# Third slots for attention scores and transposed probabilities, six temporaries, and a 1 KB transfer scratch in a five-layer transformer kernel

## The chip, the cores and the metric

One core of a Trainium2 chip runs the whole program. The metric is the device time of one execution, in microseconds; the number to compare is the median of three runs of each kernel.

## What is computed

The input is one sequence of 512 tokens with 1024 channels in float32. Four layers with post-normalisation run first: latent attention (MLA), sliding-window attention (SWA), attention with forget gates (FOX) and MLA again. A fifth, larger block follows: a short convolution, a pooling mixer, two kinds of attention with relative bias (one with a top-k choice of keys), a gated feed-forward part and a gated projection at the end.

```python
for i in range(4):                       # MLA, SWA, FOX, MLA
    y = branch[i % 3](x)                 # (softmax(q k^T) v * silu(gate)) @ w_out
    x = layernorm(ALPHA * x + y)
x = x + rmsnorm(concat(conv, pool, topk_attn, block_attn) @ w_out_2)
x = x + rmsnorm(swiglu(rmsnorm(x)))
x = x + sigmoid(rmsnorm(x) @ w_ple_gate) * (p @ w_ple_proj)
```

Each attention has 16 heads of 64 value channels in the first four layers; MLA and FOX are causal over all 512 keys, SWA sees the block before and its own.

## The kernel before, in words

Every float32 operand of a large matmul is split into a high and a low part (`split`, L183; `w`, L131, for weights), and a product is three matmuls, L157 to L159 (`mm3`). Weights come in pieces of 256 KB by DMA, issued by SyncE; ScalarE makes the high part (L138), GpSimd or VectorE the low part (L139).

A layer of the first four runs over eight pairs of heads (`pairs`, L586). For each pair the projections of the *next* pair are written first (`prep`), then the two heads of this pair, then its gate (L601), then the product of gate and result (`gated`, L465: og times u, a cast L469, a low part L470). After the eight pairs `layer_end` (L304) multiplies by the output weights, normalises and transposes; the output weights borrow free tiles: `f` for the last two pieces of the first half (L263), `qk` and one `pth`/`ptl` for the second half (`pair_units`, L266).

One head is `attend` (L390). TensorE makes the scores in PSUM tiles "s" (L157 to L159 for MLA, L238 and L239 otherwise). VectorE adds the mask or bias and finds the row maximum (L403), which writes the scores into one SBUF tile with tag "p", up to 1280 numbers a partition. ScalarE takes the exponential in place (L419), VectorE the reciprocal (L422) and the normalisation in place (L427). TensorE transposes 128x128 blocks into PSUM tiles "t" (L443), ScalarE casts them into "pth" (L184), VectorE makes "ptl" (L185), and TensorE multiplies both with the values into the PSUM tile "o" (L452). `join` (L458) adds the two halves of "o" into a tile "og" with tag "f" (L462, L463). So "p" is held from the first L403 of a head to its last L443.

Tags stand for a fixed number of slots: a tile waits until one of its tag's slots is free. The first four layers share one pool with the counts of `PH1`; the fifth block has two pools (`PH2`, `PH3`) that lie over the same memory afterwards. PSUM has 3 "acc", 2 "s", 2 "t" and 1 "o". The order of instructions on each engine is not the written order: the framework's planner (`schedule_with_timeline_sim=True`, L1133) arranges it before the run by its own timing model, from the dependences, the written order as priority and the free slots. On the chip each engine then follows that order.

```python
PS_BUFS = dict(acc=3, s=2, t=2, o=1)
sc = s.t("p", [P, sum(w)])               # L396, held to the last transpose
nc.tensor.transpose(ps[:, n:n + P], sc[:, c:c + P], s.ident)   # L443
ph = s.t("pth", [P, S], R)               # L445
```

Of the kernel before, what the change touches and what calls it, by code (L numbers as in the profile page):

```python
# [88 lines left out]
class Kern:  # L89
# [993 lines left out]
    def run(s, x, out, layers=range(4), second=True):  # L1083
        with ExitStack() as ctx:
            s.phase(ctx, PH1)
            xT = s.act(8)
# [15 lines left out]
            s.ple(hT, out)  # L1102


PH1 = dict(cqt=1, f=4, p=2, pth=2, ptl=2, qk=7, qr=1, cq=2, ckv=2, rope=2, kr=1, gq=1)
PH2 = dict(kl=2, f=6, p=2, pth=2, ptl=2, v=3, qk=4, rb=2, cw=6, pad=3, bd=2, iw=1, sel=1, sb=1, m8=3)
PH3 = dict(f=6, p=2, hid=6, hid2=2, sel=1, sb=1)

# [28 lines left out]
```

## Time and profile before

| what | us |
|---|---|
| median of 3 runs (1758.92 to 1761.11) | 1760.01 |
| the profiled execution | 1762.84 |
| its span, first to last instruction | 1761.1 |
| TensorE (PE) busy | 1684.8 |
| VectorE (DVE) busy | 962.0 |
| ScalarE (ACT) busy | 873.8 |
| GpSimd (POOL) busy | 854.4 |
| mean granted clock of TensorE | 0.979 of full |

A row of the profile names an engine, a line of the kernel and the tiles (written <- read). PE are matmuls, PEld weight loads, which run beside them. Busy time of PE is modelled from the size of each matmul, and one matmul overlaps the next, so the distance from start to start is the better measure of pace. "Idle before" is time in which the engine did nothing before an instruction, with what ended it. In the first four layers the stages are: start and latents of MLA 0 to 70 us, its heads 70 to 252, the layer's end and the projections of SWA to 316, its heads to 478, the layer's end and start of FOX to 546, its heads to 777, the same for MLA to 868, its heads to 1043, and the layer's end with the start of the fifth block to 1101.

### The profile page before, as it was taken

The page shows a single profiled execution, that of the slowest core. Times are in us where ns is not written, and L with a number is a line of the kernel's source. Part 1 is how long each engine was busy: PE and PEld are TensorE (multiplying, and loading weights), DVE is VectorE, ACT ScalarE, POOL GpSimd, SP SyncE. Part 2 cuts the span into 40 slices and gives each one's busy share as a digit, 9 for nine tenths or more (in the row PEclk, how much of TensorE's full clock was granted, in tenths as well). Part 3 has the DMA queues.
Part 4 walks back from the last instruction along what each step waited for, and adds up shares of the span by engine and source line. Part 5 has one row for each costly group of instructions (what it writes and reads, how often), then busy time and mean ns, then how long its engine had stood idle before and what let it go on. Part 6 is the DMA issues. An engine that isn't in the chain of part 4 may idle for free.

```text
span 1761.1 us, 25691 instructions
## 1 busy us (share of the span) xinstructions
PE 1684.8 (96%) x8818; PEld 1435.2 (81%) x8818; DVE 962.0 (55%) x2223; ACT 873.8 (50%) x2054; POOL 854.4 (49%) x775
## 2 busy tenths in 40 slices
PE   8999999999999999999999998999999999999999
PEld 7888878887788888778888877877778888888877
DVE  4587654677654665766587665599544222210053
ACT  4576543666445655633576642755544333332351
POOL 1644534444255665616644523745644444443571
PEclk9999999999999999999999998999999999999999
DMA  5434534322032333314444523332332333332332
GB/s 169 132 98 114 165 104 124 99 70 87 26 97 81 101 88 93 116 51 127 120 110 103 176 61 74 91 81 64 114 90 83 98 96 96 96 100 80 105 99 72
DMA packets 190339, 173.91 MB, mean 99 GB/s; under 512 B 14280, under 2 KB 154952, under 8 KB 190208
## 3 DMA queue, kind: packets, MB, share of 16 engines
q1 hardware_dynamic: 190208, 172.27, 33.9%
q8 instruction: 70, 1.15, 0.3%
q14 instruction: 61, 0.50, 0.1%
HBM read 150.94 MB, written 6.87 MB: 90 GB/s over the span
## 4 chain that ended last, share of the span: by engine, by line
PE 52%; DVE 9%; ACT 2%; issue 2%; POOL 2%; DMA 1%; SPq 0%; ACTq 0%; POOLq 0%; DVEq 0%
PE ps_acc L157 11%; PE ps_acc L158 11%; PE ps_acc L159 11%; PE ps_s L158 4%; PE ps_s L157 4%; PE ps_s L159 4%; PE ps_o L452 2%; PE ps_t L443 2%; DVE p L427 1%; DVE sel L926 1%; ACT p L419 1%; DVE m L925 1%; DVE p L403 1%; PE ps_s L238 1%; DVE ptl L185 1%
## 5 line engine op out<-in xcount | busy, mean ns | idle before, releaser
L139 POOL TENSOR_TENSOR wl<-wr,wh 128x512 fp32r<-128x512 f32 (+2 forms) x362 | 472.7, 1316 | 421.5 <-ACT wh L138 408.7
L138 ACT CAST wh<-wr 128x512 fp32r<-128x512 f32 (+2 forms) x368 | 223.6, 613 | 364.9 <-PE ps_acc L158 125.1
L157 PE MATMUL ps_acc<-act,wh 128*128 128x512 f32 (+1 forms) x880 | 331.5, 377 | 0.9 <-DVE v L620 0.8
L158 PE MATMUL ps_acc<-act,wh 128*128 128x512 f32 (+1 forms) x880 | 330.2, 375 | 0.3 <-DVE act L185 0.2
L159 PE MATMUL ps_acc<-act,wl 128*128 128x512 f32 (+1 forms) x880 | 330.1, 375 | 0.0
L157 PEld LDWEIGHTS ps_acc<-act,wh 128*128 128x128 f32 x880 | 165.6, 188 | 27.9 <-PE ps_acc L159 1.2
L159 PEld LDWEIGHTS ps_acc<-act,wl 128*128 128x128 f32 x880 | 165.3, 188 | 27.5
L158 PEld LDWEIGHTS ps_acc<-act,wh 128*128 128x128 f32 x880 | 165.4, 188 | 27.0 <-DVE act L185 0.7
L419 ACT ACTIVATE p<-p,st 128x256 f32<-128x256 f32 (+3 forms) x288 | 153.5, 537 | 32.8 <-DVE st L410 17.3
L157 PE MATMUL ps_acc<-wh,act 128*128 128x256 f32 (+3 forms) x384 | 134.5, 350 | 7.7 <-ACT act L469 3.1
L185 DVE TENSOR_TENSOR ptl<-ps_t,pth 128x512 fp32r<-128x512 f32 (+1 forms) x200 | 117.6, 597 | 38.5 <-ACT pth L184 37.7
L184 ACT CAST pth<-ps_t 128x512 fp32r<-128x512 f32 (+1 forms) x200 | 100.3, 516 | 72.5 <-PE ps_t L443 63.0
L443 PE MATMUL ps_t<-c_ident,p 128*128 128x128 f32 x672 | 116.9, 283 | 17.3 <-DVE p L427 12.4
L427 DVE TENSOR_SCALAR p<-p,st 128x256 f32<-128x256 f32 (+3 forms) x264 | 132.1, 559 | 1.8
L159 PE MATMUL ps_acc<-wh,act 128*128 128x256 f32 (+3 forms) x384 | 130.7, 341 | 0.1
L158 PE MATMUL ps_acc<-wl,act 128*128 128x256 f32 (+3 forms) x384 | 130.4, 340 | 0.0
L443 PEld LDWEIGHTS ps_t<-c_ident,p 128*128 128x128 f32 x672 | 82.0, 143 | 33.7 <-DVE p L427 13.2
L452 PE MATMUL ps_o<-pth,v 128*128 128x256 f32 (+3 forms) x288 | 90.1, 318 | 6.3 <-DVE og L463 4.4
L452 PE MATMUL ps_o<-ptl,v 128*128 128x256 f32 (+3 forms) x288 | 88.2, 335 | 4.3 <-DVE ptl L185 4.2
L157 PEld LDWEIGHTS ps_acc<-wh,act 128*128 128x128 f32 x384 | 77.8, 203 | 16.0 <-ACT act L469 3.3
L158 PEld LDWEIGHTS ps_acc<-wl,act 128*128 128x128 f32 x384 | 77.7, 202 | 5.1 <-issue 0.5
L159 PEld LDWEIGHTS ps_acc<-wh,act 128*128 128x128 f32 x384 | 77.1, 201 | 5.5 <-DVE act L185 0.3
(371 smaller groups left out, 3801.3 us busy)
## 6 DMA issues: line engine op xcount, KB each, us to landing
wr<-in_w_gate_up_dram SPq DMA_DIRECT2D x88, 256.0 KB, 2.8
wr<-in_fox_w_in_dram SPq DMA_DIRECT2D x60, 256.0 KB, 3.1
wr<-in_w_in_dram SPq DMA_DIRECT2D x48, 256.0 KB, 2.9
wr<-in_w_down_dram SPq DMA_DIRECT2D x44, 256.0 KB, 2.6
wr<-in_swa_w_in_dram SPq DMA_DIRECT2D x40, 256.0 KB, 2.9
wr<-in_mla_w_in_dram SPq DMA_DIRECT2D x32, 256.0 KB, 3.1
qk<-qk SPq DMA_DIRECT2D x32, 256.0 KB, 3.1
wr<-in_mla_w_out_dram SPq DMA_DIRECT2D x32, 256.0 KB, 3.5
```

Of the source, the lines that this page charges most:

```text
L138: nc.scalar.copy(h, raw)
L139: (nc.vector if dve else nc.gpsimd).tensor_sub(l, raw, h.bitcast(F32))
L157: mm(out, lh, rh, start=first, stop=False)
L158: mm(out, lh, rl, start=False, stop=False)
L159: return mm(out, ll, rh, start=False, stop=last)
L184: s.nc.scalar.copy(hi, src)
L185: s.nc.vector.tensor_sub(lo, src, hi.bitcast(F32))
L238: mm(out, q[:, e, c], kd[:, kk], start=True, stop=False)
L419: nc.scalar.activation(a, a, AF.Exp, bias=st[:, 1, i:i + 1], scale=scale, accum_out=st[:, 2, i:i + 1])
L427: nc.vector.tensor_scalar_mul(a, a, st[:, 3, i:i + 1])
L443: nc.tensor.transpose(ps[:, n:n + P], sc[:, c:c + P], s.ident)
L452: nc.tensor.matmul(o[:, j * P:j * P + m], vj, pp[:, c:c + m], start=first, stop=k == 1 and grp[-1] == max(2, grp[-1]) and j == grp[-1], sk ...
```

## The change

The counts of the first pool grow: `f` from four to six slots, `p`, `pth` and `ptl` from two to three. The room is taken from the reserve that the framework keeps in each SBUF partition for transfers whose addresses are computed on the way: it falls from the framework's default of 16,384 bytes to 1024. The functions of the kernel are unchanged.

```diff
-PH1 = dict(cqt=1, f=4, p=2, pth=2, ptl=2, qk=7, qr=1, cq=2, ckv=2, rope=2, kr=1, gq=1)
+PH1 = dict(cqt=1, f=6, p=3, pth=3, ptl=3, qk=7, qr=1, cq=2, ckv=2, rope=2, kr=1, gq=1)
...
-    nc = bacc.Bacc("TRN2", target_bir_lowering=False, num_devices=1)
+    nc = bacc.Bacc("TRN2", target_bir_lowering=False, num_devices=1, dynamic_dma_scratch_size=1024)
```

A slot of `f`, `pth` and `ptl` is 2 KB a partition, a slot of `p` 5 KB.

## Rows read from the trace of the kernel before

**Rows 1.** The page's part 1: busy time, share of the span and instructions of each engine.

```profile
PE 1684.8 (96%) x8818; PEld 1435.2 (81%) x8818; DVE 962.0 (55%) x2223; ACT 873.8 (50%) x2054; POOL 854.4 (49%) x775
```

**Rows 2.** Busy time by stage of the first 1101 us: stretch (us from the span's start), its length, then busy us and instructions (x) of PE, PEld, DVE, ACT and POOL, the mean granted clock of TensorE, DMA share and GB/s.

```profile
0.00:70.00 70.00, 60.60 (x344) 54.72 (x344) 30.11 (x66) 34.29 (x95) 29.96 (x43) 0.98 0.49 149
70.00:252.00 182.00, 172.93 (x935) 147.18 (x933) 127.94 (x347) 113.85 (x301) 84.94 (x78) 0.98 0.45 124
252.00:316.00 64.00, 63.00 (x371) 54.51 (x372) 29.96 (x56) 24.90 (x45) 28.07 (x21) 0.97 0.42 125
316.00:478.00 162.00, 151.82 (x796) 127.62 (x795) 119.86 (x331) 99.18 (x262) 61.10 (x47) 0.96 0.23 68
478.00:546.00 68.00, 67.12 (x410) 59.62 (x409) 33.89 (x62) 29.69 (x57) 39.29 (x39) 1.00 0.32 91
546.00:777.00 231.00, 223.45 (x1240) 193.18 (x1238) 147.60 (x368) 138.78 (x332) 127.14 (x127) 0.98 0.32 92
777.00:868.00 91.00, 87.72 (x476) 77.19 (x476) 48.15 (x88) 33.99 (x96) 54.19 (x60) 0.98 0.37 107
868.00:1043.00 175.00, 168.71 (x921) 143.54 (x919) 124.31 (x342) 109.37 (x293) 73.45 (x67) 0.99 0.43 120
1043.00:1101.00 58.00, 49.85 (x297) 45.14 (x298) 35.65 (x59) 17.36 (x36) 22.89 (x23) 0.91 0.26 64
```

**Rows 3.** Waits of PE over the whole span: who waited for whom, us in total, times, longest us.

```profile
PE ps_t L443 <- DVE p L427: 12.4, 17, 2.5
PE ps_acc L157 <- ACT act L469: 7.3, 3, 3.1
PE ps_s L238 <- DVE st L403: 5.5, 7, 1.6
PE ps_t L443 <- DVE ptl L185: 4.5, 6, 2.4
PE ps_o L452 <- DVE og L463: 4.4, 10, 0.9
PE ps_o L452 <- DVE ptl L185: 4.2, 4, 2.7
```

**Rows 4.** Timeline of one place in the heads of SWA: start us, us, engine, line, operation, tiles, shape, count, and in brackets the idle time before it with what ended it.

```profile
429.31 3.12 DVE L427 TENSOR_SCALAR p<-p,st 128x128 f32<-128x128 f32 x4
429.46 1.29 POOL L139 TENSOR_TENSOR wl<-wr,wh 128x512 fp32r<-128x512 f32 x1 [1.36 <-ACT wh L138]
...
430.95 0.44 PE L443 MATMUL ps_t<-c_ident,p 128*128 128x128 f32 x2 [0.49 <-DVE p L427]
...
432.23 0.70 PE L443 MATMUL ps_t<-c_ident,p 128*128 128x128 f32 x4 [0.84 <-DVE p L427]
...
434.52 0.33 PE L238 MATMUL ps_s<-qk 128*128 128x128 f32 x1 [1.18 <-DVE st L403]
```

**Rows 5.** The stretch after that place by busy time (columns as in rows 2), and from the timeline two weight matmuls in it and two some 38 us earlier.

```profile
434.80:441.40 6.60, 6.45 (x16) 4.81 (x16) 2.78 (x10) 2.17 (x9) 0.00 (x0) 0.50 0.40 119
...
437.15 0.63 PE L157 MATMUL ps_acc<-wh,act 128*128 128x512 f32 x1
437.58 0.63 PE L158 MATMUL ps_acc<-wl,act 128*128 128x512 f32 x1
...
398.55 0.39 PE L157 MATMUL ps_acc<-act,wh 128*128 128x512 f32 x1
398.78 0.39 PE L158 MATMUL ps_acc<-act,wh 128*128 128x512 f32 x1
```

**Rows 6.** Timeline around the first reduction of a head in the first MLA layer, in FOX and in the second MLA layer.

```profile
90.67 0.38 PE L443 MATMUL ps_t<-c_ident,p 128*128 128x128 f32 x2
91.24 0.68 DVE L403 CUSTOM_DVE_ANT_0 p<-ps_s,c_mask 128x512 f32<-128x512 f32 x1
...
686.08 0.38 PE L443 MATMUL ps_t<-c_ident,p 128*128 128x128 f32 x2
686.86 0.68 DVE L403 CUSTOM_DVE_ANT_0 p<-ps_s,rope 128x512 f32<-128x512 f32 x1
...
980.93 0.33 PE L159 MATMUL ps_s<-qk 96*128 96x384 f32 x1
982.48 0.39 PE L443 MATMUL ps_t<-c_ident,p 128*128 128x128 f32 x2
982.90 0.69 DVE L403 CUSTOM_DVE_ANT_0 p<-ps_s,c_mask 128x512 f32<-128x512 f32 x1 [0.38 <-PE ps_t L443]
```

**Rows 7.** Waits of DVE over the whole span: reductions that waited for transposes.

```profile
DVE p L403 <- PE ps_t L443: 7.2, 8, 1.9
```

**Rows 8.** The page's part 3: the queue that carries the kernel's own transfers, and the two of instructions.

```profile
q1 hardware_dynamic: 190208, 172.27, 33.9%
q8 instruction: 70, 1.15, 0.3%
q14 instruction: 61, 0.50, 0.1%
```

**Rows 9.** Waits of all engines over the whole span: two around borrowed tiles.

```profile
ACT pth L138 <- PE ps_o L452: 14.9, 5, 4.9
POOL f L139 <- DVE og L463: 14.0, 2, 8.5
```

**Rows 10.** Busy time in a stretch of the feed-forward part, columns as in rows 2.

```profile
1364.00:1584.00 220.00, 220.00 (x973) 182.15 (x972) 46.80 (x59) 71.70 (x121) 104.75 (x81) 1.00 0.33 97
```

## The prediction

> **What bounds the kernel now.** I read the page first, then busy time and clock by stage, then TensorE's waits, then single heads in the timeline. On the page TensorE (PE) is busy for 96% of the span and no other engine for over 55% [rows 1]. A gain can therefore only come from what PE loses between its matmuls, and the change can reach PE's losses only in the first four layers, whose pool it enlarges. The table by stage shows where they are [rows 2]. In the four attention stretches PE stands idle for 182 − 172.93 = 9.1 us, 162 − 151.82 = 10.2, 231 − 223.45 = 7.6 and 175 − 168.71 = 6.3: together 33 us. In the same rows the granted clock lies below 1; (1 − clock) times length gives 3.6 + 6.5 + 4.6 + 1.8 = 16.5 us of lost clock. The projections between them lose little: 1.0, 0.9 and 3.3 us.
>
> PE's own list of waits says for what [rows 3]. The longest one is for the transposes of a head's probabilities, which wait for VectorE's normalisation (L427): 12.4 us in 17 waits. The scores (L238) wait 5.5 us for VectorE's reduction (L403) to empty a PSUM bank. Then come waits at which SBUF slots play no part: the output projection waits for the last head's gated product (7.3 us), and heads wait for the PSUM tiles "o" and "t" (4.4 and 4.5 us).
>
> The timeline of one place in the sliding-window layer shows how such a wait goes on [rows 4]. Four normalisations take 3.12 us beside work of GpSimd, PE's transposes wait 0.49 and 0.84 us between them, the next scores wait 1.18 us, and from there to 441.4 the clock granted is 0.50, that is 1.2 GHz: two matmuls of 128x512 start 0.43 us apart, against 0.23 us at 2.4 GHz [rows 5].
>
> What ties two neighbouring heads together is the tag "p". A head keeps its slot from its first reduction to its last transpose, and there are two. In three heads of three layers the pattern is the same [rows 6]: the last transposes of the head before the previous one run at 90.67, 686.08 and 982.48, and the first 512-wide reduction of the new head starts 0.57, 0.78 and 0.42 us later, although in the third case its scores had left PE by 981.3. As a wait that VectorE shows, this is small (7.2 us in 8 waits [rows 7]); the planner, which orders the instructions before the run, has put other work there. It costs through the order: while a head is held back, PE has one chain fewer to turn to when the normalisation of the older one is late.
>
> **The change part by part.** *Scratch.* All of the kernel's own transfers are issued by SyncE and appear on the one queue "hardware_dynamic", with 190,208 packets; the other queues carry instructions only [rows 8]. No transfer that GpSimd would build is in the trace, so the smaller scratch takes nothing away: 0 us. It frees 15 KB a partition, and the new slots need 2 x 2 KB (f), 5 KB (p, 1280 numbers) and 2 x 2 KB (pth, ptl), 13 KB in all. No instruction or transfer is added or removed; what moves is the planned order.
>
> *Third slot of p.* It can act on the waits of L443 for L427 and of L238 for L403: 12.4 + 5.5 = 17.9 us. It shortens no chain; it gives PE another head's scores to run while one waits, and it does so only where slots were the limit, as in the three heads. The long wait chosen above lies beside a busy GpSimd and stays as long as it is, if nothing else is at hand. I take half, 9 us; bounds 0 and 17.9 for a gain, and a loss under the rivals.
>
> *Clock.* The 16.5 us come with such waits, but not only with these: the stretch of rows 5 has three of them ahead of it. I take a third, 5.5 us; bounds 0 and 16.5.
>
> *Third slots of pth and ptl.* The casts into pth (L184) wait for the transposes, which is for data. In the list a slot of pth is waited for only where the output weights borrow it (L138 behind L452, 14.9 us in 5 waits of ScalarE [rows 9]), and at that time PE has the other weights at hand. 0 us, at most the 4.2 us that L452 waits for ptl [rows 3].
>
> *Six f.* At a layer's end the last two weight pieces borrow four f, which is all there are; GpSimd then stands 14.0 us in 2 waits behind the last head's join [rows 9]. PE there waits for the gated product (7.3 us), which is late for its own chain. So 0 us; if more early gate projections were to leave PE without filling at a layer's end, the cost would be seen there.
>
> *What comes back.* Heads that follow closer press on the same one bank of "o" and two of "t", whose waits are 4.4 + 4.5 = 8.9 us now; a quarter more is +2 us (bounds 0 and 8.9).
>
> *Later stages.* The second pool's tiles lie over other tiles of the first; the hand-over, 1043 to 1101, has 8.2 us of PE idle and a clock of 0.91 [rows 2], and its waits are for the normalised rows. 0 us, ±3.
>
> Sum: −9 − 5.5 + 2 = −12.5 us. The profiled execution took 1762.8 us (span 1761.1, 1.7 outside it), 2.8 over the median of the three runs. The saving is taken off the median: 1760.0 − 12.5 = **1747.5 us**.
>
> **Weighed against a page.** In the stretch 1364 to 1584 PE has no wait at all, and its weight loads (PEld) take 182.15 of 220 us, 82.8% [rows 10]; in the attention stretches they take 80.9, 78.8, 83.6 and 82.0% [rows 2]. If that share were the ceiling, the room would be 3.5 + 6.5 + 0 + 1.4 = 11.4 us, idle and clock together, not the 49.6 counted above. The Trainium skill (Perfetto Trace Analysis, Identifying the Most-Contended Engine) holds the busy share of matmuls a poor measure and wants headroom judged by the busy share of weight loads; no row here shows which of the two is right where short transposes are mixed in. With half of 11.4 the sum would be −5.7.
>
> **The rivals.**
> *Slower: the order on VectorE.* VectorE works in the planned order. With a third slot, four reductions of a new head (0.68 us for the first, rows 6) can stand ahead of the normalisation for which PE waits. For: VectorE is at 127.94 of 182 and 119.86 of 162 us in these stretches [rows 2] and each such wait reaches PE; the planner decides by its own durations, and the 3.12 us of rows 4 are not typical. Against: older work should come first where both are ready. It decides from the point where this happens at each of the 17 waits: 17 x 0.68 = 11.6 us, and one more stretch at 1.2 GHz such as that of rows 5 (6.6 us at half, 3.3 lost): +15, **1775 us**.
> *No difference: PSUM.* The tags acc, s, t and o hold 3 + 2 + 2 + 1 tiles. A new head's scores need a free s, its result the only o, and both stay as they are. For: the waits for banks, 5.5 + 4.5 + 4.4 = 14.4 us, are above the 12.4 for the normalisation [rows 3], and VectorE seldom waits for a slot outright [rows 7]. Then the third slots lie unused: **1760 us**. The Trainium skill (Perfetto Trace Analysis, Optimization Strategy) says that bubbles which repeat can mean SBUF or PSUM is short; it does not tell which.
> *Small gain: weight loads.* The ceiling of the part before: 1760.0 − 5.7, **1754 us**.
>
> **How the numbers follow.** Forecast 0.45, weight loads 0.15, PSUM 0.16, order on VectorE 0.24. A measurement of this kernel can tell about 0.2% from no change, 3.5 us. So faster 0.60, same 0.16, slower 0.24. The range begins at all of the 17.9 us and half of the clock with nothing given back, −26: 1734. Above, it takes in PSUM and half of the loss on VectorE, +8: 1768. Left out are the rest of that loss (0.1) and clock gains beyond the half. The likeliest case alone runs from 1734 to 1756.
>
> **What would show it.** Right: in the profile after, L443's waits for L427 at 4 to 8 us, attention stretches shorter by 2 to 5 us each, sliding-window most, clock there 0.97 and up, first reductions that no longer follow the transposes of the head two before, and no change from 1364 on. Wrong: the same PE waits under another name (o, t or s banks), which is PSUM; L443's waits longer, with reductions between L422 and L427, which is VectorE; layer ends longer by what the attention saved, which would mean that filling was only used up earlier.

## The result, and the profile after

The changed kernel takes 1780.97 us (median of 4 runs, 1778.31 to 1781.87) beside 1759.47 for the kernel before: a ratio of 1.0122 [1.0104, 1.0140]. It is 21 us slower, where 12.5 less were forecast. Its profiled execution took 1781.87 us with a span of 1780.1, 19.0 more than the span before.

Page of the kernel after: the span, part 1 and the queue of the kernel's own transfers.

```profile
span 1780.1 us, 25673 instructions
...
PE 1686.4 (95%) x8818; PEld 1437.5 (81%) x8818; DVE 943.7 (53%) x2223; ACT 873.5 (49%) x2054; POOL 851.8 (48%) x775
...
q1 hardware_dynamic: 190208, 172.27, 33.9%
```

Work and transfers are those of before [rows 1, 8]. PE's busy time grew by 1.6 us and its idle time from 1761.1 − 1684.8 = 76.3 to 93.7 us, so idle time is 17.4 of the 19.0.

The kernel after by stage, cut at its own boundaries; columns as in rows 2.

```profile
0.00:74.00 74.00, 62.16 (x353) 55.71 (x353) 31.23 (x69) 34.27 (x95) 33.73 (x47) 1.00 0.51 150
74.00:256.00 182.00, 171.21 (x924) 146.06 (x924) 121.00 (x343) 113.84 (x301) 81.80 (x75) 0.98 0.45 122
256.00:320.00 64.00, 62.62 (x370) 54.70 (x371) 29.84 (x56) 24.77 (x45) 26.20 (x20) 0.97 0.40 119
320.00:486.00 166.00, 153.36 (x801) 129.39 (x799) 118.13 (x331) 99.19 (x263) 62.34 (x48) 0.95 0.23 68
486.00:555.00 69.00, 65.97 (x404) 58.78 (x405) 34.03 (x62) 29.26 (x56) 37.67 (x38) 1.00 0.31 85
555.00:787.00 232.00, 223.74 (x1240) 193.50 (x1238) 142.22 (x368) 139.46 (x333) 129.42 (x128) 0.98 0.34 93
787.00:880.00 93.00, 87.66 (x466) 77.03 (x467) 46.98 (x87) 33.41 (x95) 50.72 (x58) 0.96 0.33 99
880.00:1062.50 182.50, 171.29 (x930) 145.93 (x928) 121.35 (x344) 109.73 (x294) 75.61 (x69) 0.98 0.43 116
1062.50:1120.00 57.50, 48.78 (x302) 44.04 (x303) 35.70 (x59) 17.06 (x36) 22.45 (x22) 0.94 0.25 65
```

What was 1101 us is now 1120, and what follows is 660.1 us in both (1761.1 − 1101 and 1780.1 − 1120): the whole loss lies in the first four layers and the hand-over. Length minus PE's busy time in the four attention stretches was 33.2 us [rows 2] and is 10.8 + 12.6 + 8.3 + 11.2 = 42.9. The rest of the 17.4 lies at the layer ends (0.4, 2.2 and 2.1), the start (2.4) and the hand-over (0.6). The clock is no better: (1 − clock) times length gives 3.6 + 8.3 + 4.6 + 3.7 = 20.2 us in these stretches, after 16.5.

Waits of PE in the kernel after, over the whole span (columns as in rows 3).

```profile
PE ps_s L238 <- DVE st L403: 9.3, 11, 2.7
PE ps_t L443 <- DVE ptl L185: 8.7, 7, 2.5
PE ps_acc L157 <- ACT act L469: 8.1, 4, 2.8
PE ps_t L443 <- DVE p L427: 7.7, 9, 1.9
...
PE ps_o L452 <- DVE og L463: 5.8, 7, 1.2
PE ps_o L452 <- ACT pth L184: 5.5, 5, 2.3
...
PE ps_o L452 <- DVE ptl L185: 4.1, 5, 2.7
...
PE ps_s L157 <- DVE st L403: 1.0, 4, 0.3
```

Set beside rows 3, the wait for the normalisation fell from 12.4 to 7.7 us. The waits for banks of PSUM rose: those for "s" from 5.5 to 9.3 + 1.0, for "t" from 4.5 to 8.7, for "o" from 4.4 to 5.8. The products that wait for the cast L184 went from 1.8 (below the rows shown of before) to 5.5. Together 14.1 us came and 4.7 went. (These waits are of the whole span; the four attention stretches hold most of them.)

The tie that the prediction read from rows 6 is gone for most heads. Counted from the start of a head's first L403 and the end of its last L443, 35 of the 56 heads that have two heads before them in their layer start while both of these are still open; in the kernel before it is none. Timeline of the first MLA layer after: the first reduction of a head here runs 4.8 us ahead of the last transposes of the head two before it.

```profile
87.59 0.69 DVE L403 CUSTOM_DVE_ANT_0 p<-ps_s,c_mask 128x512 f32<-128x512 f32 x1
...
89.67 1.27 DVE L427 TENSOR_SCALAR p<-p,st 128x128 f32<-128x128 f32 x4
...
92.38 0.38 PE L443 MATMUL ps_t<-c_ident,p 128*128 128x128 f32 x2
```

One place in SWA shows what PE waits for instead. Timeline of the kernel after; columns as in rows 4.

```profile
396.17 0.42 DVE L403 CUSTOM_DVE_ANT_0 p<-ps_s,win 128x256 f32<-128x256 f32 x1
...
397.14 0.81 PE L443 MATMUL ps_t<-c_ident,p 128*128 128x128 f32 x6
...
397.72 0.36 PE L238 MATMUL ps_s<-qk 128*128 128x256 f32 x1
...
401.55 0.61 ACT L469 CAST act<-og 128x512 fp32r<-128x512 f32 x1
401.57 4.10 DVE L427 TENSOR_SCALAR p<-p,st 128x128 f32<-128x128 f32 x4
401.72 1.26 POOL L139 TENSOR_TENSOR wl<-wr,wh 128x512 fp32r<-128x512 f32 x1 [2.82 <-ACT wh L138]
402.18 0.97 ACT L184 CAST pth<-ps_t 128x512 fp32r<-128x512 f32 x2
402.82 0.54 PE L452 MATMUL ps_o<-pth,v 128*128 128x256 f32 x1 [2.32 <-ACT pth L184]
402.94 1.31 POOL L470 TENSOR_TENSOR act<-og,act 128x512 fp32r<-128x512 f32 x1
...
404.22 1.30 POOL L139 TENSOR_TENSOR wl<-wr,wh 128x512 fp32r<-128x512 f32 x1
405.60 0.41 DVE L403 CUSTOM_DVE_ANT_0 p<-ps_s,win 128x256 f32<-128x256 f32 x1
...
406.07 0.47 PE L238 MATMUL ps_s<-qk 128*128 128x128 f32 x1 [2.71 <-DVE st L403]
```

And the stretch around it by busy time (columns as in rows 2).

```profile
400.00:407.00 7.00, 1.97 (x8) 1.25 (x6) 5.77 (x12) 4.11 (x12) 3.81 (x3) 0.71 0.17 52
407.00:413.00 6.00, 5.57 (x31) 4.92 (x30) 5.23 (x16) 3.69 (x9) 0.00 (x0) 0.77 0.08 29
```

The transposes end at 397.95, but their casts start at 402.18, behind the exponentials of the next head, a weight cast and the gated product's cast on ScalarE: the first 2.32 us. Then the next head's scores wait 2.71 us for a bank "s", whose reduction stands behind 4.10 us of the older head's normalisation on VectorE. PE works for 1.97 of 7 us, and the clock granted is 0.71 and 0.77 in these two rows. The head whose scores of 397.72 hold that bank was begun at 396.17, while the two heads before it were still open, so it had taken a third slot; that gave PE nothing to do here. The wait is for one bank: the trace shows no access to the other "s" between 396.8 and 406.07, and why the waiting scores were not given that one is open.

### The profile page after: what moved, and what is told of

Its sections match the earlier page's. It is cut to its first block, busy times and chain, and to the rows that moved or that the text cites. A ratio compares the mean times of both kernels' runs of the same rounds, so it can differ in the third digit from the quotient of the medians.

```text
span 1780.1 us, 25673 instructions
## 1 busy us (share of the span) xinstructions
PE 1686.4 (95%) x8818; PEld 1437.5 (81%) x8818; DVE 943.7 (53%) x2223; ACT 873.5 (49%) x2054; POOL 851.8 (48%) x775
## 4 chain that ended last, share of the span: by engine, by line
PE 53%; DVE 8%; issue 3%; POOL 2%; ACT 2%; DMA 1%; SPq 0%; POOLq 0%; DVEq 0%; ACTq 0%
PE ps_acc L157 11%; PE ps_acc L158 11%; PE ps_acc L159 11%; PE ps_s L157 4%; PE ps_s L158 4%; PE ps_s L159 4%; PE ps_o L452 2%; PE ps_t L443 2%; DVE sel L926 1%; DVE p L427 1%; DVE m L925 1%; DVE p L403 1%; ACT p L419 1%; PE ps_s L238 1%; PE ps_s L239 1%
## 5 line engine op out<-in xcount | busy, mean ns | idle before, releaser
L157 PE MATMUL ps_acc<-act,wh 128*128 128x512 f32 (+1 forms) x880 | 332.4, 378 | 1.1 <-DVE f L606 0.9
L157 PEld LDWEIGHTS ps_acc<-act,wh 128*128 128x128 f32 x880 | 166.1, 189 | 28.4 <-DVE f L606 1.1
L185 DVE TENSOR_TENSOR ptl<-ps_t,pth 128x512 fp32r<-128x512 f32 (+1 forms) x200 | 117.1, 597 | 47.2 <-ACT pth L184 46.4
L157 PE MATMUL ps_acc<-wh,act 128*128 128x256 f32 (+3 forms) x384 | 131.0, 341 | 7.2 <-ACT act L469 2.8
L184 ACT CAST pth<-ps_t 128x512 fp32r<-128x512 f32 (+1 forms) x200 | 98.8, 519 | 72.5 <-PE ps_t L443 67.1
L159 PE MATMUL ps_acc<-wh,act 128*128 128x256 f32 (+3 forms) x384 | 128.9, 336 | 0.4 <-DVE act L185 0.4
L443 PE MATMUL ps_t<-c_ident,p 128*128 128x128 f32 x672 | 110.7, 282 | 16.8 <-DVE ptl L185 8.7
L427 DVE TENSOR_SCALAR p<-p,st 128x256 f32<-128x256 f32 (+3 forms) x264 | 123.0, 526 | 1.7
L443 PEld LDWEIGHTS ps_t<-c_ident,p 128*128 128x128 f32 x672 | 81.2, 144 | 29.4 <-issue 12.3
L157 PEld LDWEIGHTS ps_acc<-wh,act 128*128 128x128 f32 x384 | 76.1, 198 | 14.8 <-ACT act L469 3.0
L463 DVE TENSOR_TENSOR og<-ps_o,og 64x512 f32<-64x512 f32 x72 | 49.0, 681 | 59.1 <-ACT og L462 58.2
```

The lines of the kernel that those rows point to most:

```text
L157: mm(out, lh, rh, start=first, stop=False)
L159: return mm(out, ll, rh, start=False, stop=last)
L184: s.nc.scalar.copy(hi, src)
L185: s.nc.vector.tensor_sub(lo, src, hi.bitcast(F32))
L427: nc.vector.tensor_scalar_mul(a, a, st[:, 3, i:i + 1])
L463: nc.vector.tensor_add(og[a], o[:64], og[a])
```

## The experiments

The theories go by numbers in the expectations. T1: the third slot of p opens further heads, and VectorE then stands in the join (VectorE's wait of L463 behind L462 is 12.7 us before the change and 58.2 after). T2: any new order costs, whatever the cause. T3: six f use up filling early. T4: pth and ptl carry the loss. T5: TensorE's order carries it. T6: ScalarE's does. T7: no single engine's does. T8: only slots of the chain of heads (f, p, pth, ptl) cost. T9: the further heads wait for the PSUM tiles s, t and o. T10: the new order is bad whatever the banks.

**Each part alone.** Four kernels, each with the scratch of 1024 bytes:

```diff
-    nc = bacc.Bacc("TRN2", target_bir_lowering=False, num_devices=1)
+    nc = bacc.Bacc("TRN2", target_bir_lowering=False, num_devices=1, dynamic_dma_scratch_size=1024)
# scratch_only: this alone; the others, beside it, in PH1:
# p3_only: p=3      f6_only: f=6      pt3_only: pth=3, ptl=3
```

scratch_only: 

> Only the 1 KB scratch; all slot counts as before. The planned order of every engine is the same as before, only addresses differ. Both theories (T1: the third p slot; T2: any new order costs a few us) expect no change: ratio 0.998 to 1.002. If it is slower by 1%, the memory placement or the scratch is the cause and both fall.

p3_only: 

> 1 KB scratch and p=3; f, pth, ptl as before. T1 (a third scores slot lets the planner open another head ahead, heads get longer from first reduction to join, VectorE stands in the join L463 behind ScalarE's L462, TensorE loses that): nearly the whole loss, +14 to +22 us (1774 to 1782), the wait of L463 for L462 at 40 us or more against 12.7 before. T2 (each new order costs or gains a few us in an unrelated way): anything from -8 to +12 us, and the wait of L463 does not follow the time.

f6_only: 

> 1 KB scratch and f=6; p, pth, ptl as before. T1: 0 to +4 us. T3 (early gate projections use up the filling of TensorE): +8 to +20 us. T2: anything from -8 to +12.

pt3_only: 

> 1 KB scratch and pth=ptl=3; p and f as before. T1: within 4 us of before, L463's wait for L462 stays near 13 us. T4 (a third pth and ptl lets transposes run ahead of the one PSUM tile o, so that joins come later): +8 to +20 us with L463's wait at 30 us or more. T2: anything from -8 to +12.

| kernel | median us | ratio to before (1760.07) |
|---|---|---|
| scratch_only | 1761.37 | 1.0009 [0.9993, 1.0025] |
| p3_only | 1770.57 | 1.0053 [1.0035, 1.0071] |
| f6_only | 1764.05 | 1.0030 [1.0009, 1.0051] |
| pt3_only | 1768.80 | 1.0045 [1.0032, 1.0058] |

The scratch costs nothing that can be measured. Each group of slots costs something of its own, 0.53 + 0.30 + 0.45 = 1.28% against 1.22 for all: no one part carries the loss. T1 wanted 1774 to 1782 from the third p alone and nothing from pth and ptl, and missed both. T3's 8 to 20 us from six f did not come (4.0). T4's forecast for pth and ptl came true (+8.7 us, and VectorE's wait of L463 for L462 at 43.4 us), but p alone costs as much, so T4 falls as the whole cause. T2's wide range holds all three. Waits of PE with the third p alone, then with the third pth and ptl alone:

```profile
PE ps_o L452 <- DVE ptl L185: 7.8, 7, 2.7
PE ps_t L443 <- DVE ptl L185: 7.4, 4, 2.9
PE ps_s L238 <- DVE st L403: 5.9, 7, 2.9
...
PE ps_t L443 <- DVE p L427: 4.5, 7, 1.0
```

```profile
PE ps_o L452 <- DVE ptl L185: 10.4, 13, 2.7
PE ps_t L443 <- DVE ptl L185: 8.6, 6, 2.6
PE ps_t L443 <- DVE p L427: 6.1, 10, 0.9
```

Both cut the wait for the normalisation and lengthen those for the casts' second half (L185) and the bank "t", which L185 empties; rows 3 have 4.2 and 4.5 for these two. With the third p alone the two waits that were to shrink fell from 17.9 to 4.5 + 5.9 = 10.4 us, and the kernel still became slower. With the third pth and ptl alone no head starts on a third slot (0 of 56, after 33 with the third p alone): waits grow there although no more than two heads are open at once.

**The slots with the old order, and one engine held.** The program is planned twice: first with the old slots, to learn each engine's order, then with the new ones, where every instruction of a held engine is chained to the one before it in the old order. The chain is an order of issue without a wait on the chip. In the traces the held orders of TensorE, VectorE and ScalarE are those of before in every place.

```diff
+OLD = dict(PH1, f=4, p=2, pth=2, ptl=2)
+NEW = dict(OLD, f=6, p=3, pth=3, ptl=3)
+PINNED = ('PE', 'DVE', 'Activation', 'Pool', 'SP')      # order_old: all five
...
+            for name in order:
...
+                if e in last:
+                    tc.add_manual_dep(i, last[e], mybir.DependencyInfo(mybir.DependencyClass.NoSync, ...
+                last[e] = name
# pin_pe: ('PE',)   pin_dve: ('DVE',)   pin_dve_act: ('DVE', 'Activation')   pin_act: ('Activation',)
# free_act, free_dve, free_pe: all five but that one
```

order_old: 

> All slots of the changed kernel and the 1 KB scratch, but the instructions of all five engines held in the order that the planner found with the old slot counts. If the loss lies in the new order alone (T1 and T2 alike): 1752 to 1764 us, ratio 0.996 to 1.002; the reductions can no longer wait for a slot of p (7.2 us in 8 waits before), so at best a few us are gained. If the slots themselves cost (placement in memory, later stages laid over other tiles): 1770 or more.

pin_pe: 

> Changed slots; only TensorE's order held as before, the other four engines are ordered anew. T1 (the loss comes from the order of VectorE and ScalarE, with joins standing early in their queues): 1770 to 1780, L463's wait for L462 at 35 us or more. T5 (the loss comes from TensorE's order: further heads are begun and the filling is spent early): 1755 to 1765, whatever L463 waits.

pin_dve: 

> Changed slots; only VectorE's order held as before. T1: 1756 to 1765 and L463's wait for L462 back under 20 us. T5: 1770 or more, since TensorE's order differs in thousands of rows.

pin_dve_act: 

> Changed slots; VectorE's and ScalarE's order held as before, TensorE free (its order then differs in far fewer rows). T1: 1756 to 1764. T5: 1762 to 1772, between before and changed.

free_act: 

> Changed slots; TensorE, VectorE, GpSimd and SyncE hold the order of before, only ScalarE is ordered anew. T6 (ScalarE's order carries the loss: with a third pth the casts of transposes and the copies of the join stand ahead of work that is ready, and ScalarE waits at the head of its queue): 1768 to 1780. T7 (no single engine carries it, each engine's new order costs some): 1762 to 1768. If ScalarE is innocent: 1756 to 1762.

pin_act: 

> Changed slots; only ScalarE's order held as before, the other four ordered anew. T6: 1757 to 1766, against 1781 to 1784 with only TensorE or only VectorE held. T7: 1768 to 1782.

free_dve: 

> Changed slots; TensorE, ScalarE, GpSimd and SyncE hold the order of before, only VectorE is ordered anew. If VectorE's order alone carries the loss (reductions of further heads ahead of other work): 1770 to 1782. If it takes the new orders of several engines together: 1757 to 1765, as with only ScalarE anew (1760.8).

free_pe: 

> Changed slots; only TensorE is ordered anew, within what the held orders of the other four allow (its order then differs in some 790 rows). If TensorE's order carries the loss by itself: 1766 to 1776. If it takes several engines together: 1757 to 1764.

(The kernel before had medians of 1761.61, 1760.95 and 1760.65 beside them.)

| kernel | held in the old order | median us | ratio to before |
|---|---|---|---|
| order_old | all five | 1757.99 | 0.9981 [0.9969, 0.9993] |
| free_act | all but ScalarE | 1760.80 | 1.0005 [0.9989, 1.0021] |
| free_dve | all but VectorE | 1762.25 | 1.0016 [1.0002, 1.0029] |
| free_pe | all but TensorE | 1766.69 | 1.0036 [1.0022, 1.0050] |
| pin_dve_act | VectorE, ScalarE | 1766.11 | 1.0029 [1.0017, 1.0041] |
| pin_act | ScalarE | 1773.94 | 1.0067 [1.0049, 1.0086] |
| pin_pe | TensorE | 1783.53 | 1.0122 [1.0104, 1.0139] |
| pin_dve | VectorE | 1783.01 | 1.0124 [1.0107, 1.0140] |

The first row decides the main question. With the same slots and the old order the loss is gone, and the time is 0.19% under that of before, just clear of the noise: the fastest version. So the slots do no harm; the order that the planner makes with them does.

The other rows say how far one engine goes. One engine set free from the old order costs 0.24 (ScalarE), 0.35 (VectorE) or 0.55% (TensorE) against order_old, each uncertain by about 0.2; GpSimd and SyncE were not set free alone. TensorE or VectorE held alone saves nothing, ScalarE alone saves half, and VectorE and ScalarE together save three quarters (1.0029). T5 and T6 fall as whole causes, and it takes the orders of several engines together, as T7 said. Not every row fits T7: free_act came out in the range of an innocent ScalarE, and free_pe (1766.69) just inside the range of TensorE by itself, though at two fifths of the loss. Each row is also a plan of its own. With TensorE held, VectorE's order differs from that of before in 427 of 2223 places, in the changed kernel in 1187. So these rows do not give an engine's share of the changed kernel's loss.

order_old also shows what the slots alone do. Its page row, its waits of PE, and its waits of DVE:

```profile
PE 1684.6 (96%) x8818; PEld 1436.1 (82%) x8818; DVE 958.7 (54%) x2223; ACT 873.2 (50%) x2054; POOL 855.2 (49%) x775
```

```profile
PE ps_t L443 <- DVE p L427: 12.9, 20, 1.1
PE ps_s L238 <- DVE st L403: 5.7, 8, 1.6
PE ps_o L452 <- DVE ptl L185: 4.2, 4, 2.8
PE ps_o L452 <- DVE og L463: 3.9, 7, 0.9
PE ps_t L443 <- DVE ptl L185: 3.3, 4, 2.4
```

```profile
DVE og L463 <- ACT og L462: 27.6, 17, 4.7
...
DVE p L403 <- PE ps_t L443: 0.5, 1, 0.5
```

VectorE's reductions no longer wait for transposes (0.5 us, 7.2 in rows 7), yet PE's two waits that were to shrink stand at 12.9 and 5.7 us, as before [rows 3]. This does not show that the tie of rows 6 costs nothing, because the old order keeps a reduction where it was. Only 11 of the 56 heads start on a third slot, and at the first place of rows 6 the reduction still follows the transposes, by 0.56 us after 0.57:

```profile
90.24 0.38 PE L443 MATMUL ps_t<-c_ident,p 128*128 128x128 f32 x2
90.80 0.68 DVE L403 CUSTOM_DVE_ANT_0 p<-ps_s,c_mask 128x512 f32<-128x512 f32 x1
```

And the join waits 27.6 us behind L462 without any loss, twice what it did before the change: as the mark of a loss, T1's wait falls.

**Other slots, another order.** A slot more of a tag that no chain of heads holds:

```diff
-... rope=2, kr=1, gq=1)
+... rope=3, kr=1, gq=1)      # slot_rope3
+... rope=2, kr=2, gq=1)      # slot_kr2
```

slot_rope3: 

> f, p, pth and ptl as before, but a third slot for rope (tables, windows and rows of the forget gates, on no head's chain), so that the planner arranges the work anew for a reason that has nothing to do with scores. T2 (any new order costs: the old one was a good one among many): +4 to +10 us, 1764 to 1770. T8 (the loss belongs to the slots of the head chain, f, p, pth and ptl): within 3 us of before.

slot_kr2: 

> As the run before, with a second slot for kr (the rotated key of MLA, one low part in FOX). T2: +4 to +10 us, 1764 to 1770. T8: within 3 us of before.

Measured: 1761.92 us, 1.0001 [0.9989, 1.0013], and 1760.74 us, 1.0003 [0.9989, 1.0018], beside 1760.95. Both are planned anew: compared place by place in the traces (line, tiles and shape of each of the 8818 matmuls), TensorE's order differs from that of before in 1021 and 1104 places, after the change in 3061, and in free_pe, which costs 0.55% more than order_old, in only 436. So these two new orders are free, and the amount of reordering is no measure of its cost. T2 falls, as far as two orders can tell; T8 holds for the two tags tried.

**More PSUM.** One bank of "acc" becomes a third "s" (s3) or "t" (t3), each with the old slots and with the new ones; the three places that name a third "acc" at once use the new bank:

```diff
-PS_BUFS = dict(acc=3, s=2, t=2, o=1)
+PS_BUFS = dict(acc=2, s=3, t=2, o=1)      # t3: acc=2, s=2, t=3, o=1
...
-    (["acc", "acc", "acc", "o"], ["s", "s", "s", "s"]),
+    (["acc", "acc", "s", "o"], ["s", "s", "s", "s"]),      # and so in L384 and L872; t3: "t"
```

s3_old: 

> PSUM moved: three s tiles and two acc instead of two and three; f, p, pth, ptl as before, 1 KB scratch. One acc less costs by itself: 1760 to 1780 is open under every theory; it is the base for the next run.

s3_new: 

> As the run before, with the slots of the change. T9 (the further heads that the new slots admit wait for PSUM: s, t and o): with a third s the step from old to new slots falls from +21 to +10 us or less, and TensorE's waits for L403 in front of scores to 4 us or less. T10 (the new order is bad whatever the banks): the step stays at +15 to +25.

t3_old: 

> PSUM moved: three t tiles and two acc; f, p, pth, ptl as before, 1 KB scratch. The base for the next run, 1760 to 1780.

t3_new: 

> As the run before, with the slots of the change. T9: the wait of transposes for L185, 4.5 us before and 8.7 in the changed kernel, under 3 us, and the step from old to new slots +12 us or less. T10: the step stays at +15 to +25.

| kernel | median us | ratio to before (1761.03) |
|---|---|---|
| s3_old | 1839.18 | 1.0434 [1.0398, 1.0471] |
| s3_new | 1817.64 | 1.0324 [1.0306, 1.0343] |
| t3_old | 1837.48 | 1.0435 [1.0415, 1.0456] |
| t3_new | 1821.60 | 1.0353 [1.0330, 1.0375] |

The exchange costs over 4%. Under it the same step from old to new slots saves 21.5 and 15.9 us, where with three "acc" it costs 21. So the sign depends on the banks, as T9 said (+10 and +12 us or less), and T10 (+15 to +25) falls. In detail T9 did less well. With the third "t" the wait of L443 for ptl is 1.5 us, as it should be:

```profile
PE ps_t L443 <- DVE ptl L185: 1.5, 2, 0.7
```

With the third "s" the wait of L238 for L403 is 6.9 us, and should have been at most 4 (waits of PE in s3_new):

```profile
PE ps_s L238 <- DVE st L403: 6.9, 9, 2.1
```

And a kernel with two "acc" and no further bank was not run. So whether it is the spare bank that makes the slots pay, or the scarcer filling from "acc", stays open.

Nor do the banks stand behind every such loss. In pin_pe TensorE issues exactly the order of before, and the loss is as large (1.0122). Waits of PE there:

```profile
PE ps_t L443 <- DVE p L427: 15.0, 20, 1.1
...
PE ps_o L452 <- DVE og L463: 6.5, 8, 2.7
...
PE ps_s L238 <- DVE st L403: 3.9, 6, 1.2
...
PE ps_t L443 <- DVE ptl L185: 3.3, 4, 2.4
```

With 3.1 us of L157 for L403, the waits for s, t and o come to 16.8 us: near the 14.4 of before, and far from the 24.8 of the changed kernel.

## Why the prediction was wrong, step by step

- **Where the time can move: right.** All of it moved in the first four layers and the hand-over.
- **Scratch, 0 us: right.** 1.0009 [0.9993, 1.0025].
- **Third slot of p, −9 us: this step failed.** The planner did use the slot (35 of 56 heads), and the sign for the longest wait came true: L443 behind L427 stands at 7.7 us where 4 to 8 was written. But the term counted the scores' wait for L403 among the gains, and that grew, so that the two waits together went from 17.9 to only 7.7 + 9.3 = 17.0 us. Where they did fall nearly as forecast, by 7.5 us with the third p alone, the kernel became 0.53% slower. So the step from "PE waits less for the normalisation" to "the kernel takes less time" is the one that failed: PE lost more at other waits of the new order. What the slots give without a new order is 3.6 us for all of them (1761.61 to 1757.99), and the profile does not say at which wait. Whether the tie of rows 6 cost anything by itself was not isolated.
- **What comes back, +2 us: this term failed with it, too small and too narrow.** 14.1 us came back. The waits for "o" and "t" went from 8.9 to 14.5 us, +5.6 and inside the bounds. The banks "s" (+4.8) and the casts L184 (+3.7) were not in the term at all. With the 4.7 saved, PE's waits in the heads come to +9.4 us, near the +9.7 of idle time of the attention stretches. The other 7.7 us of idle time, at the start, the layer ends and the hand-over, were put at nothing.
- **Clock, −5.5 us: wrong.** It was to follow fewer waits; there were more, and the lost clock went from 16.5 to 20.2 us.
- **pth and ptl, 0 us, and f, 0 us: wrong.** They cost 0.45% and 0.30% alone. The reason given was that only weight pieces at a layer's end wait for such slots, where PE does not need them. But a slot count is an input of the planner, and the order changes elsewhere too: with six f alone PE's wait of L576 for L571 goes from 2.3 to 6.7 us.
- **Later stages, 0 us: right.** Hand-over 58.0 to 57.5 us, the rest 660.1 in both.
- **Rivals.** The order on VectorE had the sign, and a size near the result (+15 us). Its mechanism was not seen: L443's wait for L427 grew shorter, not longer; at the place shown the reductions stand *behind* the normalisation; and holding VectorE's order alone saves nothing (1.0124). What is left of it is its premise, that the planned order decides, and that VectorE's order has a part in it: held together with ScalarE's it saves three quarters. The PSUM rival named the place where PE now waits, s, t and o, but took it that the slots would lie unused. The ceiling of weight loads was not tested: their share fell in all four attention stretches (80.3, 77.9, 83.4 and 80.0% after), so the loss came from idle time, not from loads. Its room was also too small: the differences of shares times the lengths give 11.4 us, but the lengths less the loads' time at a share of 82.8% give 4.2 + 7.9 + 0 + 1.6 = 13.7 us, and half of it 6.9. On the rule that the prediction names beside the PSUM rival (the Trainium skill, Perfetto Trace Analysis, Optimization Strategy: repeated bubbles can mean that SBUF or PSUM is short) the runs say that SBUF slots of the heads alone, with the order held, are worth 0.19% here.

**Shown and not shown.** Shown: the new order costs the time, and the slots do not (order_old beside the change); not every new order costs (slot_kr2, slot_rope3); no engine's order, set free or held alone, accounts for all of it (TensorE, VectorE and ScalarE tried). Read from the profile of the changed kernel, and supported by the change of sign under other banks, but not isolated: that further open heads press on the same s, t and o. Against it as the whole cause stands pin_pe. Open: which rows of the new order cost most, each engine's share, and what of s3 and t3 comes from the missing "acc".

## What to carry to other kernels

Where a planner orders the instructions, a slot count is also an input of the order: time it once with the old order held, and once planned anew, before it is judged. A slot that the limiting engine never waits for can still cost. And a shorter wait in the profile is not yet saved time: add up what the other waits of that engine do. That more heads in flight need more of the other things that each holds, here PSUM banks, is likely from the profile and was not isolated.

## What the runs showed that was not expected

The same slots moved the time by −0.19% or by +1.22%, with the same instructions and transfers, by their order alone. One bank of "acc" less, with a further "s" or "t" in its place, costs 4.3%, more than anything in the change. And the four normalisations of a head in SWA (128 and three times 256 numbers a partition) took 4.10 us in the place shown and 3.12 in rows 4, those of a head in MLA with more numbers (128, 256, 384 and 512) only 1.27 in the row at 89.67. The trace shows what goes with it: work of GpSimd. In the first 1120 us after the change, the 67 normalisations of 256 numbers with no GpSimd instruction beside them take 0.34 to 0.35 us each, the 29 beside one 0.85 on average and up to 1.39. At the place shown the three of 256 take 1.35 or 1.36 us each, beside the three GpSimd instructions at 401.72, 402.94 and 404.22. The reductions L403 of the same width, which read PSUM, take 0.39 to 0.43 us with or without. No run took the GpSimd work away, so what it would save is open.
